# Gate and up of two chunks per feed-forward block as seven block products instead of eight

## The chip, the core and the metric

The kernel runs on one core of a Trainium2 chip. Its engines are TensorE (in the profile PE, with its weight loads as PEld), VectorE (DVE), ScalarE (ACT), GpSimd (POOL) and SyncE (SP), which here only issues the transfers of weights. The metric is the device time of one execution in microseconds (us); lower is better.

## The reference, cut to what matters

Two layers, each with a feed-forward block, a mixer (latent attention with a recurrence in the first layer, differential attention in the second), and a second feed-forward block: four feed-forward blocks in all. The sequence has 256 tokens of width 1024; all inputs are fp32.

```python
def swiglu(x, w_gate, w_up, w_down):
    return (jax.nn.silu(x @ w_gate) * (x @ w_up)) @ w_down
...
    h = swiglu(rms_norm(x, g[0, 0]), ffn_w_gate[l, 0], ffn_w_up[l, 0], ffn_w_down[l, 0])
    x = x + 0.5 * rms_norm(h, g[0, 1])
```

`w_gate` and `w_up` are [1024, 2816], `w_down` is [2816, 1024], and each block has its own.

## The kernel before, in words

**Tiles.** The 256 tokens are two row tiles (t = 0, 1) of 128. The operand of a block stands in SBUF transposed, `xT[t]`, eight k tiles of [128, 128]. An fp32 product is made of three fp32r products: every value is split in a high part, `hi`, and a rest, `lo`, and `mm3` (lines 242 to 246) issues hi times hi, hi times lo and lo times hi, each a matmul of 512 columns into one PSUM bank.

**The weight stream.** All weights are stored in the order of use and pass through SBUF in subunits of [128, 1024] fp32 (512 KB). `emit_load` (line 197) emits for each: the transfer into a tile `raw` (pool of 5), the copy to `hi` by ScalarE (line 219) and the rest `lo` = `raw` - `hi` by VectorE (line 224), the rests in the order of the stream. In a feed-forward block the pairs `hi`, `lo` take 7 places of a pool of the block's own (`BUFS_F`); subunits that are emitted ahead of the block's opening take the 5 places of the pool `wsp`. `fill` (line 256) keeps about seven subunits emitted ahead of TensorE.

**A feed-forward block** (`ffn`, line 430) goes over the 2816 columns in chunks of 512, 512, 256, 512, 512, 512. A chunk of 512 takes four subunits of gate and four of up, each of two k tiles; each subunit serves both row tiles: 2 tiles x 2 k tiles x 3 = 12 matmuls. Then ScalarE computes silu of gate, VectorE the product with up (`gated`, line 445), and one chunk later `turn` (line 448) transposes the result and splits it to `hT`, and `down` (line 454) multiplies it with four subunits of down, 12 matmuls each, into the four banks `y`. Chunk 0 is made by `group_first` (line 275): row tile 0 first, while the second tile's operand is still being normalised and transposed; chunks 1 to 5 by `group`. After the last chunk, `finish` (line 403) normalises the block's output and makes the next operand.

**Order.** The program is written once, unrolled; a scheduler places each engine's instructions in an order by priority (norms and the splits of transposes ahead), and each engine then runs its queue in that order. GpSimd has only small work in these blocks: one power of a [128, 1] column per norm (lines 343 and 388).

Of the kernel before, what the change touches and what calls it, by code (L numbers as in the profile page):

```python
# [20 lines left out]
P = 128  # L21
D = 1024
# [12 lines left out]
BUFS_F = 7  # L35
CHUNKS = [512, 512, 256, 512, 512, 512]

# ---------------------------------------------------------------- weight stream
# A unit is (name, index, first k tile, k tiles, column ranges): [128, k tiles, columns],
# stored contiguously in the order of use.  # L40


def _ffn_units(l, j):
# [12 lines left out]
    for ci, (a, w) in enumerate(starts):  # L56
        step = 2048 // w
        for k in range(0, KD, step):
# [54 lines left out]
for _i in range(1, len(UNITS)):  # L113
    if UNITS[_i - 1][0].endswith("w_out") and not UNITS[_i][0].endswith("w_out"):
        BLOCK_OF[_i - 1] = BLOCK_OF[_i]
        MOVED.add(_i - 1)
# [6 lines left out]
def _pack(inputs):  # L123
    parts = []
    for name, idx, k0, nk, cols in UNITS:
# [6 lines left out]
# ---------------------------------------------------------------- constants of the shapes  # L132
# [37 lines left out]
def forward(ctx, tc, a):  # L170
# [19 lines left out]
    # ------------------------------------------------------------ weight stream  # L190
    SPLIT = 1024
    state = {"i": 0, "off": 0, "block": -1, "pool": None, "first": None, "n": 0}
# [3 lines left out]

    def emit_load():
        if state["i"] >= len(UNITS):
            return
        u = UNITS[state["i"]]  # L200
        pool, tag = (state["pool"], "f") if BLOCK_OF[state["i"]] == state["block"] else (wsp, "w")
# [3 lines left out]
        off = state["off"]  # L205
        state["off"] += P * width
        src = a["w"][off:off + P * width].rearrange("(p n) -> p n", p=P)
        nc_ = width // nk
        per = max(1, SPLIT // nc_)
        for k in range(0, nk, per):  # L210
            n = min(per, nk - k)
            w = n * nc_
            raw = wraw.tile([P, SPLIT], F32, name="raw", tag="raw")
            moved = nc.sync.dma_start(raw[:, :w], src[:, k * nc_:k * nc_ + w])
            if state["n"] in late:
                after(late[state["n"]](), moved)
# [13 lines left out]
    def take(nk):  # L230
        """The next subunits that make up nk k tiles."""
# [10 lines left out]
    def mm3(ps, lhs, j, rhi, rlo, start, stop):  # L242
        hi, lo = lhs
        mm(ps, hi[:, j, :], rhi, start=start, stop=False)  # L244
        mm(ps, hi[:, j, :], rlo, start=False, stop=False)  # L245
        state["mm"] = mm(ps, lo[:, j, :], rhi, start=False, stop=stop)  # L246
# [16 lines left out]
    def group(pss, lhss, n, nk=KD, k0=0):  # L263
        """pss[t][:, :n] = lhs_t^T @ the next weight group [nk*128, n]; a step of side work after each subunit."""
# [46 lines left out]
    # ------------------------------------------------------------ start  # L311
# [19 lines left out]
    def after(b, a_):  # L331
        """b is issued after a_ (on one engine)."""
# [5 lines left out]
    def rpow(ss, n, mul, add):  # L338
        """(ss * mul + add) ** -0.5"""
# [6 lines left out]
    def to_T(src, dst, n, j0=0, bank=bank):  # L346
        """dst[(hi, lo)][:, j0:j0+n, :] = transposes of the n 128-column blocks of src."""
# [15 lines left out]
    def turn_x(t, xg):  # L363
        """Closures: halves of xT[t] = xg^T, split."""
# [11 lines left out]
    def post_norm(t, ys, g, half, gnext):  # L376
        """x[t] += (0.5 if half) rms(y) g; returns xg = x[t] * gnext."""
# [40 lines left out]
    # ------------------------------------------------------------ FFN  # L418
    def ffn_scope(block):
        """Opens the pools of an FFN; its weights go to them from here on."""  # L420
# [6 lines left out]
        state["tmp"] = lambda: fp.tile([P, 512], F32, name="tmp", tag="h")  # L427
        return fx, fp, fr

    def ffn(scope, r, turn1, gpost, gnext, at=None):  # L430
        fx, fp, fr = scope
        with fx:
# [21 lines left out]
            def down(t, subs, first, last, k0=0, banks=(0, 1)):  # L454
                """y[t] += h^T ^T @ the down weights; first/last: the f tile that opens/closes the sum."""
                for hi, lo, m, _ in subs:
# [4 lines left out]
                    k0 += m  # L461

# [10 lines left out]
            h = [gated(t, pu[t], s[t], w) for t in range(NT)]  # L473
            for ci in range(1, nch):
                w, wp = CHUNKS[ci], CHUNKS[ci - 1]
                pg = [bank(), bank()]
# [41 lines left out]
    # ------------------------------------------------------------ rope tables  # L518
# [39 lines left out]
    def rope(v, tab, w, pool):  # L558
        """v [P, n, 2w] in place; tab [P, 2, 2w] = (cos cos), (-sin sin)."""
# [13 lines left out]
    # ------------------------------------------------------------ output projection of a mixer  # L573
# [46 lines left out]
    def even(r, turn1, tab, lb, lbm):  # L620
        with ExitStack() as ex:
# [23 lines left out]
            def turn4(src, dst, rows=P, w=P, copy=None, bank=bank):  # L645
                """dst [rows, 4, P] = transposes of the four w-column blocks of src."""
# [5 lines left out]
            # ---- latent q and rope part of k  # L652
# [29 lines left out]
            # ---- latent kv  # L682
# [14 lines left out]
            # ---- forget gate  # L697
# [471 lines left out]
```

## Time and profile before

| | |
|---|---|
| device time, median of 3 runs | 1028.74 us (1028.34 to 1030.66) |
| span of the profiled execution, first to last instruction | 1027.8 us |
| PE busy | 1011.3 us, 98% of the span, 4979 matmuls |
| DVE busy | 625.8 us, 61% |
| ACT busy | 517.1 us, 50% |
| POOL busy | 49.9 us, 5% |
| weight stream, mean of all transfers | 179 GB/s |

The profiled execution has no time of its own beside its span; the median of the runs is 0.94 us above the span. Matmuls are pipelined, so their listed durations overlap; the rate of TensorE is read from start to start. [...]

### The profile page before, as it was taken

What the parts mean: (1) busy time and instruction counts of PE and PEld (TensorE: products, weight loads), DVE (VectorE), ACT (ScalarE), POOL (GpSimd) and SP (SyncE); (2) the same over time, 40 slices, a digit from 0 to 9 for tenths busy, and PEclk for the clock granted to TensorE, in tenths of its full rate; (3) what the DMA queues carried; (4) which work ended last, traced back from release to release, by engine and by line L of the source; (5) the groups of instructions that cost most, each with busy time, mean ns of one, the idle gap of its engine ahead of it and who ended that gap; (6) DMA issues with size and microseconds to landing.
All of it is one profiled execution on the core that took longest, in us unless ns stands there. A gap on an engine that the chain in (4) does not pass through costs nothing.

```text
span 1027.8 us, 13158 instructions
## 1 busy us (share of the span) xinstructions
PE 1011.3 (98%) x4979; PEld 843.5 (82%) x4979; DVE 625.8 (61%) x876; ACT 517.1 (50%) x757; POOL 49.9 (5%) x61
## 2 busy tenths in 40 slices
PE   8999999999999999999999999999999999999997
PEld 6888888888788889888888888888877878888886
DVE  6555585768577855455576555546676786455553
ACT  6544455477644644444554444444665565444441
POOL 1000000021201000000000000000011200000000
PEclk8999999999999999999999999999999999999999
DMA  8765555575221765555547555555634366655531
GB/s 282 271 202 186 186 184 189 180 225 194 86 81 58 253 212 196 185 184 187 182 164 246 187 183 189 191 190 168 208 121 147 102 206 225 201 182 189 186 123 41
DMA packets 51903, 184.25 MB, mean 179 GB/s; under 512 B 6136, under 2 KB 6528, under 8 KB 51840
## 3 DMA queue, kind: packets, MB, share of 16 engines
q1 hardware_dynamic: 48960, 176.05, 51.8%
q10 hardware_dynamic: 2880, 7.37, 2.1%
q8 instruction: 39, 0.64, 0.2%
q14 instruction: 24, 0.20, 0.1%
HBM read 182.35 MB, written 1.05 MB: 178 GB/s over the span
## 4 chain that ended last, share of the span: by engine, by line
PE 90%; DVE 4%; issue 3%; ACT 1%; DMA 1%; POOL 1%; SPq 0%; DVEq 0%; POOLq 0%; ACTq 0%
PE w L244 16%; PE w L246 16%; PE w L245 16%; PE y L246 9%; PE y L244 9%; PE y L245 9%; PE w L292 7%; PE w L353 2%; DVE wlo L224 1%; PE y L353 1%; DMA raw<-in_w_dram 1%; ACT whi L219 1%; POOL pm L1007 0%; DVE E L857 0%; DVE pm L1009 0%
## 5 line engine op out<-in xcount | busy, mean ns | idle before, releaser
L224 DVE TENSOR_TENSOR wlo<-raw,whi 128x1024 fp32r<-128x1024 f32 (+2 forms) x331 | 404.0, 1227 | 283.6 <-ACT whi L219 281.2
L219 ACT CAST whi<-raw 128x1024 fp32r<-128x1024 f32 (+1 forms) x331 | 345.0, 1049 | 365.5 <-PE w L246 206.6
L244 PE MATMUL w<-whi,xThi 128*128 128x512 f32 (+1 forms) x836 | 315.6, 377 | 0.0
L246 PE MATMUL w<-whi,xTlo 128*128 128x512 f32 (+1 forms) x836 | 312.0, 373 | 0.0
L245 PE MATMUL w<-wlo,xThi 128*128 128x512 f32 (+1 forms) x836 | 311.5, 373 | 0.0
L246 PEld LDWEIGHTS w<-whi,xTlo 128*128 128x128 f32 x836 | 157.3, 188 | 28.3 <-issue 0.3
L244 PEld LDWEIGHTS w<-whi,xThi 128*128 128x128 f32 x836 | 157.5, 188 | 27.5 <-issue 1.0
L245 PEld LDWEIGHTS w<-wlo,xThi 128*128 128x128 f32 x836 | 157.5, 188 | 26.4
L244 PE MATMUL y<-whi,hThi 128*128 128x512 f32 x352 | 138.4, 393 | 0.0
L246 PE MATMUL y<-whi,hTlo 128*128 128x512 f32 x352 | 137.2, 390 | 0.0
L245 PE MATMUL y<-wlo,hThi 128*128 128x512 f32 x352 | 137.1, 389 | 0.0
L246 PEld LDWEIGHTS y<-whi,hTlo 128*128 128x128 f32 x352 | 66.1, 188 | 14.0
L245 PEld LDWEIGHTS y<-wlo,hThi 128*128 128x128 f32 x352 | 66.1, 188 | 13.2
L244 PEld LDWEIGHTS y<-whi,hThi 128*128 128x128 f32 x352 | 66.1, 188 | 13.2
L361 DVE TENSOR_TENSOR hTlo<-w,hThi 128x512 fp32r<-128x512 f32 (+1 forms) x48 | 29.1, 640 | 34.0 <-ACT hThi L360 34.0
L440 ACT ACTIVATE s<-w,sm 128x512 f32<-128x512 f32 (+1 forms) x48 | 31.4, 653 | 25.9 <-PE w L246 20.3
L388 POOL TENSOR_TENSOR sm<-sm,mhalf 128x1 f32<-128x1 f32 x12 | 6.6, 550 | 726.6 <-DVE sm L386 726.6
L292 PE MATMUL w<-whi,xThi 128*128 128x512 f32 (+2 forms) x124 | 39.1, 397 | 2.6 <-ACT xThi L360 2.6
L292 PE MATMUL w<-wlo,xThi 128*128 128x512 f32 (+2 forms) x124 | 37.8, 389 | 0.4 <-DVE wlo L224 0.4
L292 PE MATMUL w<-whi,xTlo 128*128 128x512 f32 (+2 forms) x124 | 37.9, 390 | 0.0
L445 DVE SCALAR_TENSOR_TENSOR h<-w,sm,s 128x512 f32<-128x512 f32 (+1 forms) x48 | 32.0, 699 | 0.7 <-PE w L246 0.5
L292 PEld LDWEIGHTS w<-whi,xThi 128*128 128x128 f32 x124 | 22.6, 192 | 6.6 <-ACT xThi L360 3.1
(246 smaller groups left out, 820.2 us busy)
## 6 DMA issues: line engine op xcount, KB each, us to landing
raw<-in_w_dram SPq DMA_DIRECT2D x325, 512.0 KB, 3.6
g<-in_norm_g_dram ACTq DMA_DIRECT2D x9, 512.0 KB, 4.6
raw<-in_w_dram SPq DMA_DIRECT2D x4, 448.0 KB, 3.4
g<-in_norm_g_dram SPq DMA_DIRECT2D x2, 512.0 KB, 6.2
out_dram<-x SPq DMA_DIRECT2D x4, 256.0 KB, 2.1
E<-in_hw_dram ACTq DMA_DIRECT2D x1, 576.0 KB, 6.7
x<-in_x_dram SPq DMA_DIRECT2D x2, 256.0 KB, 3.0
x<-in_x_dram SPq DMA_DIRECT2D x1, 512.0 KB
```

What stands on the lines that cost most here:

```text
L219: c = nc.scalar.copy(hi[:, :w], raw[:, :w])
L224: state["lo"] = nc.vector.tensor_tensor(lo[:, :w], raw[:, :w], hi[:, :w].bitcast(F32), op=ALU.subtract)
L244: mm(ps, hi[:, j, :], rhi, start=start, stop=False)
L245: mm(ps, hi[:, j, :], rlo, start=False, stop=False)
L246: state["mm"] = mm(ps, lo[:, j, :], rhi, start=False, stop=stop)
L292: state["mm"] = mm(o, lhs[:, k, :], rhs[:, i, :], start=j == 0 and k == 0, stop=j == 2 and k == KD - 1)
L353: nc.tensor.transpose(ps[:, i * P:(i + 1) * P], src[:, (b + i) * P:(b + i + 1) * P], ident)
L361: return c, nc.vector.tensor_tensor(lo.rearrange("p a b -> p (a b)"), ps, h2.bitcast(F32), op=ALU.subtract)
L388: nc.gpsimd.tensor_tensor(r, v, mhalf[:, :1], op=ALU.pow)
L440: nc.scalar.activation(s[:, :w], ps[:, :w], AF.Silu, scale=r[t])
L445: nc.vector.scalar_tensor_tensor(hh[:, :w], ps[:, :w], r[t], s[:, :w], op0=ALU.mult, op1=ALU.mult)
```

## The change: what it does

In chunks 1 and 3 of each block (`SEVEN = (1,3)`), gate and up are taken as one product of 2 x 2 blocks: row tile times half of k, and half of k times {gate, up}, each block of weights [512, 512]. Strassen's scheme in Winograd's form makes it from seven block products (`prod`, 12 matmuls each) instead of eight:

- Four sums of rows of the operand, `row_sums`, once per block after chunk 0: twelve GpSimd operations on [128, 512] (four re-additions of `hi` and `lo`, four sums, four rests) and four ScalarE copies. Both chunks use them.
- Four sums of weights per chunk (T1 to T4), each of two subunits: eight VectorE operations on [128, 1024], made in place in the `raw` tiles, which come from a pool of 8 of their own.
- Each of the seven weight blocks is split as before: 14 subunits with `hi` and `lo` instead of 8. A subunit now serves one product, 6 matmuls instead of 12.
- The products are added in PSUM where they can be (banks X, W, Y), with three ScalarE copies (`held`) and three VectorE sums (`plus`) per chunk for the rest.
- The down products of the chunk before are taken between the products T3 and T4 and after B22.
- The pairs `hi`, `lo` of a block take, by turns (`RING`), the 5 places of `wsp` and 4 of the block's own: 9 in all.

```diff
-BUFS_F = 7
+BUFS_F = 4
+SEVEN = (1,3)
+RAWS = 8
+RING = "wfwfwfwfw"
...
+        if ci in SEVEN:
+            gate, up = ([("ffn_w_" + n, (l, j), k, 4, [(a, a + w)]) for k in (0, 4)] for n in ("gate", "up"))
...
+            units += [gate[0] + ("B11",), up[0] + ("T1",), up[1] + ("T2",), gate[1] + ("B21",), (None, None, 0, 4, [(a, a + w)], "T3")]
+            units += d[:half] + [(None, None, 0, 4, [(a, a + w)], "T4"), (None, None, 0, 4, [(a, a + w)], "B22")] + d[half:]
+            continue
...
+                raw = (wraw if kind is None else state["raws"]).tile([P, SPLIT], F32, name="raw", tag="raw")
...
+                sub = nc.vector.tensor_tensor
+                if kind in ("B11", "B21"):
+                    kept[kind, k] = raw
+                elif kind == "T1":
+                    sub(raw, raw, kept["B11", k], op=ALU.subtract)
+                    kept["T", k] = raw
+                elif kind == "T2":
+                    kept["B22", k] = raw
+                    sub(kept["T", k], raw, kept["T", k], op=ALU.subtract)
+                    raw = kept["T", k]
+                elif kind == "T3":
+                    raw = kept["B11", k]
+                    sub(raw, kept["T", k], raw, op=ALU.subtract)
+                elif kind == "T4":
+                    raw = kept["B21", k]
+                    sub(raw, raw, kept["T", k], op=ALU.subtract)
+                else:
+                    raw = kept["B22", k]
+            pool, tag = wsp, "w"
+            if ours:
+                if RING[state["turn"] % len(RING)] == "f":
+                    pool, tag = state["pool"], "f"
+                state["turn"] += 1
...
+            def row_sums(fp):
+                xf = [cp.tile([P, D], F32, name="xf", tag="c") for _ in range(NT)]
+                A = [[xf[t][:, 512 * i:512 * i + 512] for i in range(2)] for t in range(NT)]
+                tt = nc.gpsimd.tensor_tensor
+                for t in range(NT):
+                    for i in range(2):
+                        hi, lo = (v.rearrange("p k n -> p (k n)").bitcast(F32) for v in half(t, i))
+                        tt(A[t][i], hi, lo, op=ALU.add)
+                tt(A[1][1], A[1][0], A[1][1], op=ALU.add)
+                tt(A[1][0], A[0][0], A[1][0], op=ALU.subtract)
+                tt(A[0][0], A[1][1], A[0][0], op=ALU.subtract)
+                tt(A[0][1], A[0][1], A[0][0], op=ALU.subtract)
...
+                for v, dst in zip((A[1][1], A[0][0], A[1][0], A[0][1]), (oT[0], oT[1], *more)):
+                    hi, lo = (d.rearrange("p k n -> p (k n)") for d in dst)
+                    nc.scalar.copy(hi, v)
+                    tt(lo, v, hi.bitcast(F32), op=ALU.subtract)
...
+                X = bank()
+                prod(X, half(0, 0), True)
+                hT = [turn(0, CHUNKS[ci - 1]), None]
+                W = bank()
+                prod(W, S1, True)
+                p1 = held(X)
+                hT[1] = turn(1, CHUNKS[ci - 1])
+                prod(X, S2, False)
+                Y = bank()
+                prod(Y, half(0, 1), True)
+                u2 = held(X)
+                s0 = silu(0, plus(p1, Y), 512)
+                prod(X, S3, False)
+                downs(range(kf))
+                u3 = held(X)
+                c22 = plus(u3, W)
+                prod(X, half(1, 1), False)
+                s1 = silu(1, X, 512)
+                prod(W, S4, False)
+                h = [gated(0, plus(u2, W), s0, 512), gated(1, c22, s1, 512)]
+                downs(range(kf, wp))
...
+            sums = row_sums(fp)
             for ci in range(1, nch):
                 w, wp = CHUNKS[ci], CHUNKS[ci - 1]
+                if ci in SEVEN:
+                    seven(ci)
+                    continue
```

## Rows read from the trace of the kernel before

**Rows 1.** The page, part 1: busy us, share of span, instructions of each engine.

```profile
PE 1011.3 (98%) x4979; PEld 843.5 (82%) x4979; DVE 625.8 (61%) x876; ACT 517.1 (50%) x757; POOL 49.9 (5%) x61
```

**Rows 2.** The page, part 4: the chain that ended last, by engine.

```profile
PE 90%; DVE 4%; issue 3%; ACT 1%; DMA 1%; POOL 1%; SPq 0%; DVEq 0%; POOLq 0%; ACTq 0%
```

**Rows 3.** Timeline of PE, a gate group: start us, us, instruction, count [idle before].

```profile
450.90 0.39 PE L244 MATMUL w<-whi,xThi 128*128 128x512 f32 x1
...
461.78 1.03 PE L353 MATMUL w<-ident,h 128*128 128x128 f32 x8
462.57 0.47 PE L244 MATMUL w<-whi,xThi 128*128 128x512 f32 x1
```

**Rows 4.** Groups by shape: busy us, mean ns of one | idle before, releasers.

```profile
L224 DVE TENSOR_TENSOR wlo<-raw,whi 128x1024 fp32r<-128x1024 f32 x325 | 398.3, 1231 | 283.6 <-ACT whi L219 281.2
L219 ACT CAST whi<-raw 128x1024 fp32r<-128x1024 f32 x325 | 340.2, 1053 | 362.0 <-PE w L246 206.6 <-PE y L246 101.9 <-issue 24.5
...
L360 ACT CAST hThi<-w 128x512 fp32r<-128x512 f32 x40 | 21.7, 588 | 4.7 <-PE w L353 4.6
...
L385 DVE TENSOR_TENSOR c<-y,g 128x512 f32<-128x512 f32 x12 | 8.2, 684 | 6.1 <-ACT junk L383 6.1
```

**Rows 5.** Timeline of PE at the third feed-forward block's start and its chunk 1.

```profile
530.77 0.62 PE L292 MATMUL w<-whi,xThi 128*128 128x512 f32 x2
...
553.50 0.39 PE L244 MATMUL w<-whi,xThi 128*128 128x512 f32 x1
```

**Rows 6.** Timeline of DVE in the same block, around chunks 0 and 1.

```profile
539.31 0.69 DVE L361 TENSOR_TENSOR xTlo<-y,xThi 128x512 fp32r<-128x512 f32 x1 [2.10 <-ACT xThi L360]
541.21 6.90 DVE L224 TENSOR_TENSOR wlo<-raw,whi 128x1024 fp32r<-128x1024 f32 x6 [1.20 <-ACT whi L219]
...
554.97 1.40 DVE L445 SCALAR_TENSOR_TENSOR h<-w,sm,s 128x512 f32<-128x512 f32 x2
...
565.78 1.29 DVE L361 TENSOR_TENSOR hTlo<-w,hThi 128x512 fp32r<-128x512 f32 x2 [1.61 <-ACT hThi L360]
```

**Rows 7.** Timeline of ACT at the same place.

```profile
539.17 2.00 ACT L219 CAST whi<-raw 128x1024 fp32r<-128x1024 f32 x2
```

**Rows 8.** Timeline of POOL in the first mixer: two places with dense operands.

```profile
234.80 1.37 POOL L709 TENSOR_TENSOR E<-lb,E 128x512 f32<-128x512 f32 x1
...
307.95 2.61 POOL L909 TENSOR_TENSOR G<-G,gout 128x512 f32<-128x512 f32 x2 [1.17 <-ACT G L908]
```

**Rows 9.** Timeline of DVE at the same two places.

```profile
234.93 2.32 DVE L224 TENSOR_TENSOR wlo<-raw,whi 128x1024 fp32r<-128x1024 f32 x1
...
307.87 0.28 DVE L857 TENSOR_TENSOR E<-E,hqT 128x128 f32<-128x128 f32 x1
308.07 1.37 DVE L857 TENSOR_TENSOR E<-E,hkT 128x128 f32<-128x128 f32 x1
309.36 1.35 DVE L857 TENSOR_TENSOR E<-E,hqT 128x128 f32<-128x128 f32 x1
```

**Rows 10.** Groups by shape, POOL alone, the dense [128, 512] operations.

```profile
L909 POOL TENSOR_TENSOR G<-G,gout 128x512 f32<-128x512 f32 x2 | 2.6, 1326 | 1.2 <-ACT G L908 1.2
L708 POOL TENSOR_TENSOR E<-E,lbm 128x512 f32<-128x512 f32 x2 | 2.6, 1290 | 4.8 <-DVE kk L707 4.8
```

**Rows 11.** Windows: stretch, length, busy us (count) by engine, PEclk, DMA share, GB/s.

```profile
530.77:545.34 14.57, 14.57 (x69) 12.04 (x68) 9.39 (x14) 8.90 (x13) 1.10 (x2) 1.00 0.31 111
545.34:553.50 8.16, 8.16 (x37) 6.76 (x36) 5.21 (x5) 3.92 (x4) 0.00 (x0) 1.00 0.96 306
...
553.50:576.30 22.80, 22.80 (x106) 18.96 (x105) 13.86 (x14) 10.96 (x13) 0.00 (x0) 1.00 0.71 235
```

**Rows 12.** Windows and timeline of PE at the program's start.

```profile
9.00:12.00 3.00, 2.57 (x6) 1.50 (x7) 3.00 (x4) 2.46 (x3) 0.00 (x0) 0.50 1.02 419
...
8.92 1.18 PE L292 MATMUL w<-whi,xThi 128*128 128x512 f32 x2 [2.64 <-ACT xThi L360]
...
16.73 0.62 PE L292 MATMUL w<-whi,xTlo 128*128 128x512 f32 x2
```

More of the change, by code (lines that the diff above doesn't have):

```diff
@@ L113 @@
 for _i in range(1, len(UNITS)):
-    if UNITS[_i - 1][0].endswith("w_out") and not UNITS[_i][0].endswith("w_out"):
+    if (UNITS[_i - 1][0] or "").endswith("w_out") and not (UNITS[_i][0] or "").endswith("w_out"):
         BLOCK_OF[_i - 1] = BLOCK_OF[_i]
@@ L191, in forward @@
     SPLIT = 1024
-    state = {"i": 0, "off": 0, "block": -1, "pool": None, "first": None, "n": 0}
+    state = {"i": 0, "off": 0, "block": -1, "pool": None, "first": None, "n": 0, "turn": 0}
     queue = []
@@ L195, in forward @@
     late = {}
+    kept = {}
     def emit_load():
@@ L200, in emit_load @@
         u = UNITS[state["i"]]
-        pool, tag = (state["pool"], "f") if BLOCK_OF[state["i"]] == state["block"] else (wsp, "w")
+        ours = BLOCK_OF[state["i"]] == state["block"]
         state["i"] += 1
@@ L204, in emit_load @@
         nk = u[3]
-        off = state["off"]
-        state["off"] += P * width
-        src = a["w"][off:off + P * width].rearrange("(p n) -> p n", p=P)
+        kind = u[5] if len(u) > 5 else None
+        if u[0] is not None:
+            off = state["off"]
+            state["off"] += P * width
+            src = a["w"][off:off + P * width].rearrange("(p n) -> p n", p=P)
         nc_ = width // nk
@@ L212, in emit_load @@
             w = n * nc_
[L213 to L216, printed above, removed]
+            if u[0] is not None:
+                raw = (wraw if kind is None else state["raws"]).tile([P, SPLIT], F32, name="raw", tag="raw")
+                moved = nc.sync.dma_start(raw[:, :w], src[:, k * nc_:k * nc_ + w])
+                for key in [key for key in late if key <= state["n"]]:
+                    after(late.pop(key)(), moved)
+            if kind is not None:
+                sub = nc.vector.tensor_tensor
[21 more added lines that the diff above has]
+                state["turn"] += 1
             hi = pool.tile([P, SPLIT], F32R, name="whi", tag=tag + "hi")
@@ L461, in down, with half @@
                     k0 += m
+            def half(t, i):
+                return tuple(v[:, 4 * i:4 * i + 4, :] for v in xT[t])
+            def row_sums(fp):
[10 more added lines that the diff above has]
+                tt(A[0][1], A[0][1], A[0][0], op=ALU.subtract)
+                more = [tuple(fp.tile([P, 4, P], F32R, name=f"S{n}{i}", bufs=1) for n in ("hi", "lo")) for i in range(2)]
+                out = []
+                for v, dst in zip((A[1][1], A[0][0], A[1][0], A[0][1]), (oT[0], oT[1], *more)):
+                    hi, lo = (d.rearrange("p k n -> p (k n)") for d in dst)
+                    nc.scalar.copy(hi, v)
+                    tt(lo, v, hi.bitcast(F32), op=ALU.subtract)
+                    out.append(dst)
+                return out
@@ new lines, in prod, with seven, held, plus @@
+            def prod(ps, lhs, start):
+                k0 = 0
+                while k0 < 4:
+                    fill()
+                    hi, lo, m, _ = queue.pop(0)
+                    for i in range(m):
+                        k = k0 + i
+                        mm3(ps, lhs, k, hi[:, i, :], lo[:, i, :], start and k == 0, k == 3, not start)
+                    k0 += m
+                    pump()
+            def seven(ci):
+                nonlocal h, hT
+                wp = CHUNKS[ci - 1] // P
+                kf = (wp // 2 + 1) // 2 * 2 if ci < nch - 1 else 0
+                wp = wp if ci < nch - 1 else 0
+                S1, S2, S3, S4 = sums
+                def held(ps):
+                    c = fp.tile([P, 512], F32, name="u", tag="u", bufs=2)
+                    nc.scalar.copy(c, ps)
+                    return c
+                def plus(c, ps):
+                    nc.vector.tensor_tensor(c, ps, c, op=ALU.add)
+                    return c
+                def downs(ks):
+                    for k in ks:
+                        sub = take(1)
+                        for t in range(NT):
+                            down(t, sub, 0 if ci == 1 else None, None, k)
+                X = bank()
[19 more added lines that the diff above has]
+                downs(range(kf, wp))
```

19 lines of the change are left out of this document (13 added, 6 removed).

## The prediction

> **What bounds the kernel now.** I read the page's first part before anything else: TensorE is busy for 1011.3 of 1027.8 us, VectorE for 61%, ScalarE for 50%, GpSimd for 5% [rows 1]. The chain that ended last says the same with more weight: 90% of it is TensorE [rows 2]. Busy time alone does not say whether TensorE runs at its pace, so the next view is its timeline: 48 matmuls of a gate group lie between 450.90 and 461.78, start to start 10.88 / 48 = 0.2267 us, and the eight transposes behind them cost 0.79 us [rows 3]. That is a dense queue at granted clock 1.00. A matmul taken out is worth 0.227 us, as long as weights keep arriving split. Who makes them: per subunit one ScalarE copy of 1.05 us and one VectorE rest of 1.23 us [rows 4], against the 12 x 0.227 = 2.72 us that TensorE needs for a subunit. Both engines mostly wait; VectorE's rests wait for the copy, the copies for TensorE to free a place [rows 4].
>
> **What is removed.** Each of two chunks in each of four blocks loses one block product of 12 matmuls: 12 x 0.2267 = 2.72 us a chunk, 5.44 a block, 21.8 in all. Nothing is added on TensorE: matmuls and transposes keep their shapes.
>
> **What is added, on VectorE.** In a chunk of seven products a subunit feeds 6 matmuls, 1.36 us of TensorE. VectorE owes for it a rest, and for the eight subunits of T1 to T4 a sum as well. I price the sum like the rest, both being fp32 with two operands in SBUF: six rests back to back took 6.90 us, so (6.90 - 1.22) / 5 = 1.135 us a step [rows 6]. A sum and a rest are then 2.27 us against TensorE's 1.36: here VectorE is the slower engine, and what counts is how far ahead it enters. I do the ledger for the third block, whose operation times I have.
>
> TensorE's side: chunk 0 starts at 530.77, chunk 1 at 553.50 [rows 5]. B11, T1, T2, B21 take 4 x 2.72 = 10.88, the transposes 0.79, the first subunit of T3 1.36; the second subunit of T3 is due at 553.50 + 13.03 = 566.53.
>
> VectorE's side: at 541.21 the rests of the block's subunits begin again, with the sixth, because its copy (done at 541.17 [rows 7]) needs the place of the first, in use until row tile 1 has passed it. Numbered from 0, subunits 5 to 17 need 13 rests. Of the six sums to T3 I take the two of T1 as done earlier: VectorE idles 2.10 and 1.20 us there [rows 6], and their weights can have landed, since the transfers ran at 111 GB/s in 530.77:545.34 and reached 306 behind it [rows 11]. That leaves 17 x 1.135 = 19.30; then the gated products 1.40 and the two splits 1.29 [rows 6], and one `plus`, priced at 0.68 like a sum from PSUM [rows 4]. Together 22.67: done at 563.88, 2.65 us early. If no T1 sum is early, it is 0.4 us early. So without GpSimd the saving survives, barely.
>
> **What is added, on GpSimd, decides.** Twelve operations on [128, 512] a block, on an engine that is idle there. The trace shows what such an operation does to its neighbour. At 307.95 two of them take 2.61 us [rows 8]; of the VectorE products beside them, 0.28 us each, two take 1.37 and 1.35 [rows 9]. At 234.80 one of 1.37 us runs [rows 8], and the weight rest started at 234.93 takes 2.32 us instead of 1.23 [rows 4, 9]. Each GpSimd operation takes about 1.09 us from a VectorE operation with two operands in SBUF, and rests and sums are all of that kind. GpSimd's own length is 1.29 to 1.33 us [rows 10]. The bounds are 0 (all in VectorE's waits) and 12 x 1.09 = 13.1 us a block. I take nine, 9.8 us: the two re-additions of row tile 0 and the first of row tile 1 can run before 541.21, the others need the last half of `xT[1]` (539.31 + 0.69 [rows 6]) and fall on the stretch of the ledger. So T3 is late by 9.81 - 2.65 = 7.16 us, and the block changes by 7.16 - 5.44 = +1.7; break-even lies at (2.65 + 5.44) / 9 = 0.90 us an operation.
>
> Behind T3 nothing more is lost: four rests, two sums and two rests of T4 and B22 and one sum, 8 x 1.135 + 0.68 = 9.8 us, stand against 1.36 + 5.44 + 2.72 + 1.36 = 10.9 of TensorE. Chunk 3 uses the same row sums; before it lies chunk 2 with 22 us of TensorE for some 15 of VectorE, so I cost it at nothing. Cover gone, it would cost what chunk 1 does without GpSimd.
>
> [...]
>
> **Smaller edits.** ScalarE gets 6 copies a chunk (6.3 us), three held copies (3 x 0.59 [rows 4]) and once four copies of row sums; it was busy for 10.96 of 22.80 us there [rows 11], so it is not the slower one: 0, at most what VectorE's order adds. Transfers keep their bytes; 8 raw tiles of their own let SP issue them earlier: 0, between -1 and +1 a block. Held copies lie beside a product or down products (2.72 us or more for 0.59): 0. At the three block ends with a successor the next block's first pairs share the five `wsp` places with the last down subunits, and two early GpSimd operations meet the norm's VectorE work: I take one operation's worth, +1 us each, between 0 and 2. In the first block the tables of angles, some small VectorE work, move from beside chunk 3's end toward its start, since a chunk of seven steps 14 times and not 8: 0 to 3, taken 0.
>
> **The sum.** Four blocks x 1.7 = +6.9, three ends x 1 = +3.0. On the profiled span: 1027.8 + 9.9 = 1037.7; the runs' median lies 0.94 above that span, so 1038.6. The ends: no meeting on the port and no loss at ends, 1028.7 - 21.8 = 1007; all twelve meet and no sum is early, 13.1 - 0.4 - 5.44 = +7.3 a block and 2 an end, 1064.
>
> **Rivals.**
> A, faster: GpSimd's operations fall into VectorE's waits. For: VectorE is busy only 13.86 of 22.80 us there now [rows 11]. Against: those waits are what the new sums fill, and both begin when `xT[1]` is there. Then 1028.7 - 21.8 + 3 = 1010; 1007 to 1020.
> B, level: fewer meet. With seven, T3 is late by 7.63 - 2.65 = 4.98, the block at -0.5, in all 1030; 1022 to 1031.
> C, clearly slower: the lateness comes in one piece and TensorE's clock falls. The program's start shows it: 2.64 us of idle, then a granted clock of 0.50, two matmuls in 1.18 us at 8.92 and in 0.62 again at 16.73 [rows 12]. At half rate from 8.92 to 16.2, 7.3 us, TensorE loses 3.6; four times is 14.5: 1038.6 + 14.5 = 1053. It decides if one wait of TensorE in chunk 1 passes about 2.6 us: a gated product queued on VectorE behind sums that wait, with the transposes behind it. Against: if each subunit waits about 1 us, the clock stays, as with the 0.79 us of short transposes. [...]
> D, that the change doesn't do what it says: then TensorE would not have 4979 - 96 = 4883 matmuls. I see nothing for it.
>
> **Chances.** Forecast 0.42 (1031 to 1047, itself), A 0.30, B 0.13, C 0.15. A is all faster; B splits 0.03 faster, 0.06 level, 0.04 slower; of the forecast 0.03 is level. Faster by over 0.2% (2 us, about what a measurement of this kernel can tell from no change) 0.33, within 0.09, slower 0.58. The range runs from A's middle to C's, 1010 to 1053, which leaves about 0.2 outside.
>
> **What would show it.** Right: TensorE idle in chunk 1 of each block, ended by VectorE's rests, sums or gated products, about 7 us a block; rests and sums beside GpSimd of about 2.3 us; chunk 3 dense. Wrong: GpSimd's row sums beside VectorE operations of plain length; TensorE waiting as long in chunk 3 as in chunk 1; waits that end with a transfer or a ScalarE copy whose source had long been there.

## The result, and the profile after

The changed kernel takes 1067.68 us (median of 4 runs, 1067.12 to 1068.34) against 1028.97 for the kernel before (4 runs on the same chip, 1028.34 to 1030.66): 1.0371 times as long, 95% interval 1.0355 to 1.0388. The forecast was 1038.6, with a range from 1010 to 1053. The direction was right, the size was not: +38.7 us in place of +9.9. The profiled execution of the changed kernel has a span of 1065.7 us, 37.9 more than before.

The page's first part, which answers to [rows 1], and the chain by engine, which answers to [rows 2]:

```profile
PE 1005.6 (94%) x4883; PEld 833.1 (78%) x4883; DVE 805.3 (76%) x1012; ACT 582.9 (55%) x845; POOL 151.1 (14%) x109
...
PE 69%; DVE 15%; issue 7%; DMA 3%; ACT 3%; POOL 2%; SPq 0%; DVEq 0%; POOLq 0%; ACTq 0%
```

TensorE has 96 matmuls fewer, as it should (rival D is out), but its share of the chain fell from 90% to 69%. Where, the windows of the third block show, chunks 0 to 3 (stretch, length, busy us and count of PE, PEld, DVE, ACT, POOL, then granted clock, which is the share of TensorE's full clock in the records, DMA share, GB/s), first before (its chunk 0 is in [rows 11], in two pieces), chunks 1 to 3:

```profile
553.50:587.06 33.56, 33.56 (x153) 27.85 (x152) 19.75 (x19) 15.18 (x17) 0.00 (x0) 1.00 0.67 222
587.06:610.34 23.28, 23.28 (x153) 21.39 (x152) 11.88 (x12) 10.22 (x12) 0.00 (x0) 1.00 0.54 181
610.34:638.04 27.70, 27.70 (x126) 22.91 (x124) 14.33 (x14) 12.36 (x14) 0.00 (x0) 1.00 0.57 190
```

then after, chunks 0 to 3:

```profile
552.74:577.55 24.81, 22.96 (x105) 18.72 (x104) 21.62 (x17) 13.67 (x20) 18.38 (x12) 1.00 0.46 149
577.55:618.79 41.24, 33.13 (x142) 27.11 (x140) 39.06 (x36) 23.79 (x28) 5.70 (x3) 0.88 0.53 179
618.79:642.07 23.28, 23.28 (x154) 21.39 (x152) 22.55 (x24) 12.06 (x14) 0.00 (x0) 1.00 0.36 136
642.07:667.05 24.98, 24.98 (x113) 20.62 (x112) 20.50 (x20) 19.55 (x23) 0.00 (x0) 1.00 0.56 189
```

Chunk 3 has its 2.72 us to the last digit. Chunk 1 is 7.7 us longer, with VectorE busy for 39.06 of 41.24 and the clock at 0.88. The same cut through all four blocks (start of a chunk's first product to start of the next chunk's), summed, against the terms of the forecast:

| us against before | forecast | measured |
|---|---|---|
| chunk 3 | -10.9 | -10.6 |
| chunk 1 | 4 x (7.16 - 2.72) = +17.8 | +33.7 |
| chunk 0, mixers, start | +3.0 | +10.7, +0.5, +1.6 |
| all the rest | 0 | +2.0 |
| sum | +9.9 | +37.9 |

In chunk 1 the extra is of two kinds. Waits of TensorE add 34.6 us (four long ones, 10.0, 8.3, 8.3 and 7.2 us above a matmul's step, and a short one), and matmuls slower than 0.3 us from start to start, most of them behind a wait, add 8.1; against that stand 10.9 us saved, and 1.9 lie in smaller steps. This is the long wait in the third block, on PE's timeline:

```profile
580.05 0.39 PE L293 MATMUL w<-whi,xTlo 128*128 128x512 f32 x1
588.54 1.08 PE L400 MATMUL w<-ident,h 128*128 128x128 f32 x4 [8.11 <-DVE h L494]
```

After the first product of the chunk, 2.7 us into it, TensorE wants the transposes of chunk 0's `h`, and `h` is not there. VectorE's timeline over the same time says why:

```profile
564.76 15.15 DVE L271 TENSOR_TENSOR wlo<-raw,whi 128x1024 fp32r<-128x1024 f32 x7 [0.70 <-ACT whi L266]
579.83 4.50 DVE L249 TENSOR_TENSOR raw<-raw 128x1024 f32<-128x1024 f32 x2
584.25 1.21 DVE L253 TENSOR_TENSOR raw<-raw 128x1024 f32<-128x1024 f32 x1
585.39 2.35 DVE L271 TENSOR_TENSOR wlo<-raw,whi 128x1024 fp32r<-128x1024 f32 x2
587.66 1.40 DVE L494 SCALAR_TENSOR_TENSOR h<-w,sm,s 128x512 f32<-128x512 f32 x2
```

Seven rests take 15.15 us, 2.16 a step, where six took 6.90 before [rows 6]. Behind them the two sums of T2, a sum of T3 and two rests stand ahead of the two gated products in VectorE's queue. GpSimd's timeline beside it:

```profile
565.51 2.15 POOL L525 TENSOR_TENSOR xf<-xf 128x512 f32<-128x512 f32 x1
...
574.33 4.49 POOL L534 TENSOR_TENSOR oTlo<-xf,oThi 128x512 fp32r<-128x512 f32 x2
578.79 4.46 POOL L534 TENSOR_TENSOR Slo<-xf,Shi 128x512 fp32r<-128x512 f32 x2
```

Beside the rests each operation of the row sums takes 2.15 to 2.25 us, and one VectorE step goes by in the same time. And the granted clock around the wait (windows, columns as above):

```profile
580.00:588.00 8.00, 0.44 (x2) 0.01 (x1) 8.00 (x6) 5.41 (x6) 3.25 (x2) 0.67 0.00 0
588.00:590.00 2.00, 1.46 (x6) 1.39 (x7) 2.00 (x3) 0.34 (x1) 0.00 (x0) 0.50 0.00 0
590.00:592.00 2.00, 2.00 (x7) 1.51 (x6) 1.90 (x3) 1.20 (x2) 0.00 (x0) 0.50 0.00 0
592.00:594.00 2.00, 2.00 (x9) 1.58 (x8) 2.00 (x3) 0.00 (x0) 0.00 (x0) 0.75 0.00 0
594.00:596.00 2.00, 2.00 (x13) 1.71 (x11) 1.27 (x3) 1.51 (x3) 0.00 (x0) 1.00 0.77 233
```

TensorE comes back at a granted clock of 0.50 and gets 1.00 again some 5 us later. The DMA share is 0 through the wait and for some five more microseconds: no transfer runs. The waits of SyncE, which issues the transfers, name the reason (575 to 602: us in total, times, longest):

```profile
SPq L237 <- DVE wlo L271: 24.8, 5, 21.9
```

For 21.9 us in one piece the next transfer waits for a rest on VectorE, that is, for a raw tile to come free.

### The profile page after: what moved, and what is told of

It reads as the page before. It is cut to its first block, busy times and chain, and to the rows that moved or that the text cites. A ratio compares the mean times of both kernels' runs of the same rounds, so it can differ in the third digit from the quotient of the medians.

```text
span 1065.7 us, 13235 instructions
## 1 busy us (share of the span) xinstructions
PE 1005.6 (94%) x4883; PEld 833.1 (78%) x4883; DVE 805.3 (76%) x1012; ACT 582.9 (55%) x845; POOL 151.1 (14%) x109
## 4 chain that ended last, share of the span: by engine, by line
PE 69%; DVE 15%; issue 7%; DMA 3%; ACT 3%; POOL 2%; SPq 0%; DVEq 0%; POOLq 0%; ACTq 0%
PE w L291 13%; PE w L293 12%; PE w L292 12%; DVE wlo L271 8%; PE y L291 7%; PE y L293 7%; PE y L292 7%; DMA raw<-in_w_dram 3%; PE w L339 3%; PE w L400 2%; ACT whi L266 1%; PE w L1010 1%; DVE x L441 1%; DVE raw L249 1%; POOL sm L390 1%
## 5 line engine op out<-in xcount | busy, mean ns | idle before, releaser
L271 DVE TENSOR_TENSOR wlo<-raw,whi 128x1024 fp32r<-128x1024 f32 (+2 forms) x379 | 488.6, 1315 | 119.5 <-ACT whi L266 117.2
L266 ACT CAST whi<-raw 128x1024 fp32r<-128x1024 f32 (+2 forms) x379 | 391.2, 1048 | 281.9 <-PE w L293 106.4
L291 PE MATMUL w<-whi,xThi 128*128 128x512 f32 (+1 forms) x676 | 252.7, 374 | 1.0 <-ACT s L489 1.0
L293 PE MATMUL w<-whi,xTlo 128*128 128x512 f32 (+1 forms) x676 | 249.5, 369 | 0.0
L292 PE MATMUL w<-wlo,xThi 128*128 128x512 f32 (+1 forms) x676 | 249.2, 369 | 0.0
L291 PEld LDWEIGHTS w<-whi,xThi 128*128 128x128 f32 x676 | 127.4, 189 | 22.8 <-ACT s L489 1.2
L293 PEld LDWEIGHTS w<-whi,xTlo 128*128 128x128 f32 x676 | 127.3, 188 | 22.1 <-issue 0.3
L292 PEld LDWEIGHTS w<-wlo,xThi 128*128 128x128 f32 x676 | 127.5, 189 | 20.4
L293 PEld LDWEIGHTS y<-whi,hTlo 128*128 128x128 f32 x352 | 66.1, 188 | 14.3
L400 PE MATMUL w<-ident,h 128*128 128x128 f32 x176 | 27.0, 286 | 33.2 <-DVE h L494 26.1
L408 DVE TENSOR_TENSOR hTlo<-w,hThi 128x512 fp32r<-128x512 f32 (+1 forms) x48 | 29.8, 643 | 33.2 <-ACT hThi L407 33.1
L407 ACT CAST hThi<-w 128x512 fp32r<-128x512 f32 (+1 forms) x48 | 25.2, 554 | 52.1 <-PE w L400 52.1
```

Of the source, the lines that this page charges most:

```text
L266: c = nc.scalar.copy(hi[:, :w], raw[:, :w])
L271: state["lo"] = nc.vector.tensor_tensor(lo[:, :w], raw[:, :w], hi[:, :w].bitcast(F32), op=ALU.subtract)
L291: mm(ps, hi[:, j, :], rhi, start=start, stop=False, skip_group_check=again)
L292: mm(ps, hi[:, j, :], rlo, start=False, stop=False, skip_group_check=again)
L400: nc.tensor.transpose(ps[:, i * P:(i + 1) * P], src[:, (b + i) * P:(b + i + 1) * P], ident)
L407: c = nc.scalar.copy(h2, ps)
```

## The experiments

Theory V: VectorE, slowed by the row sums on GpSimd, has too much to do before chunk 1. Rivals: the order of the queues alone (O, later Q), late weights and the rings of places (W, R). All times are medians of four runs or more beside runs of the kernel before, in brackets the 95% interval of the ratio. "Chunk 1" and the like are sums over the four blocks against before.

**Which part makes it.**

Chunk 3 alone with seven products:

```diff
-SEVEN = (1,3)
+SEVEN = (3,)
```

> SEVEN = (3,): chunk 1 goes back to eight products, chunk 3 keeps seven, the row sums stay on GpSimd at the block's start. In the trace of the changed kernel chunk 1 is +7.4 to +9.5 us a block against before (33.9 in all), chunk 3 -2.5 to -2.72 (10.7 in all), chunk 0 and the block starts +12 in all. Theory V (VectorE, slowed by GpSimd's row sums, is late for chunk 1): chunk 1 returns to 33.6 us in each block, chunk 3 stays at 24.98, the starts keep their +12 because the twelve GpSimd operations still lie there: 1029 - 10.7 + 12 = 1030. Theory S (the starts are longer through the shared ring of pairs and the earlier demand of chunk 1 of seven, not through GpSimd): starts back to before, 1029 - 10.8 = 1018. If the shared row sums or the ring hurt later chunks too: above 1040.

1058.19 us, 1.0272 (1.0254 to 1.0290). Neither V nor S, but the case named last: chunk 3 gives its 10.6, and chunk 1, which has eight products again and the matmuls of before, is still 25.0 us longer. So chunk 1 needs no sums of weights of its own for a loss there.

No row sums:

```diff
-            sums = row_sums(fp)
+            sums = [half(0, 0), half(0, 1), half(1, 0), half(1, 1)]
```

> The row sums are left out: products S1 to S4 take the four halves of the operand as they stand, so gate and up of chunks 1 and 3 are not the reference's; all matmuls, weight sums, rests and rings stay. Theory V: without twelve GpSimd operations VectorE gets back about 12 x 1.03 = 12 us a block between chunk 0 and chunk 1 (its rest went from 1.135 to 2.16 us a step beside them), more than the 8 to 10 us by which the transposes waited; the wait goes, the clock stays, the starts lose their +12: 1068 - 34 - 10 - 12 = about 1010, at most 1020. Theory O (VectorE's order alone: the gated product stands behind the sums of T2 and T3 whatever GpSimd does): the three operations ahead of it still cost 3 x 1.135 + 2 x 1.17, so a wait of 3 us or more per block and the clock's fall stay: 1035 to 1045. Theory W (weights land late, places in the rings): nothing much changes, above 1050.

1024.61 us, 0.9946 (0.9931 to 0.9962). Chunk 1 is 7.6 us shorter than before, so 41.2 shorter than in the changed kernel: V. This edit takes the four ScalarE copies of the row sums out as well; but in the changed kernel VectorE works without a gap up to the gated products of chunk 0 (in the third block from 564.76 to 587.66, in the others as long), so these copies did not hold it up there. The total stays above V's 1020 because chunk 0 (+7.1) and the mixers (+3.3) did not come back, which neither theory had said.

Four of the twelve GpSimd operations left out:

```diff
-                    tt(lo, v, hi.bitcast(F32), op=ALU.subtract)
-                    out.append(dst)
+                    out.append((dst[0], half(0, 0)[1]))
```

> The changed kernel with eight GpSimd operations a block instead of twelve: the rests of the four row sums are left out (products S1 to S4 take a half of the operand's rest in their place, so gate and up of chunks 1 and 3 are not the reference's). Theory V (each operation takes 1.04 us of VectorE, and all of it is TensorE's wait): 4 x 1.04 x 4 blocks = 16.6 us back, and more where a wait becomes short enough for the clock to stay: 1043 to 1051. Theory O (the order of VectorE's queue decides, the last operations come too late to matter): above 1060.

1050.82 us, 1.0195 (1.0167 to 1.0222), as V said. Chunk 1 gives back 18.1 us, 1.1 for each of the 16 operations, and here the ScalarE copies stay. All 48 together, with the copies, gave 41.2, 0.86 each.

The twelve operations on VectorE:

```diff
-                tt = nc.gpsimd.tensor_tensor
+                tt = nc.vector.tensor_tensor
```

> The twelve row-sum operations run on VectorE instead of GpSimd, nothing else changes. Theory V: on GpSimd they took about 12 us from VectorE; on VectorE they cost 12 x 0.69 = 8.3 us (the price of a 512-column operation there). VectorE gains 4 us a block, some of it also at the starts, 12 to 20 us in all: 1048 to 1056. Theory O: VectorE has 8.3 us more to do in the same order, and no partner was slowing it: 1068 + 4 x 8 = 1100.

1042.87 us, 1.0138 (1.0105 to 1.0172): 24.8 us better than on GpSimd, more than V said. Chunk 1 is +17.9, chunk 0 +2.4. The engine that was to be spared is better off doing the work itself. The transposes hardly wait for the gated products any more (1.6 us in one wait); what is left in chunk 1 is mostly the row sums being late for the second product, S1: TensorE waits for their ScalarE copies `oThi` three times, 10.9 us in all.

**Order or work.** The T2 sums behind the gated products:

```diff
+            for b in sums2[-2:]:
+                after(b, state["h"])
             sums = row_sums(fp)
```

> The two sums of T2 in each chunk of seven, and what follows them on VectorE, are ordered behind the gated products of the chunk before; the work is the same. Theory O (order alone): the transposes no longer wait, all of the 34 us of long waits and the 10 us of half clock go: 1068 - 44 = 1024 to 1030. Theory V (VectorE has 7 us a block too much work before T3, wherever it stands): the wait moves from the transposes to the products of T2 and T3. VectorE was busy without a pause from 564.76 to about 594 in the third block; T3's second rest could not come before 597.5, against 590.4 when it would be due without the wait: 7.1 us late as before, so only the share of the clock can come back, up to 2.4 us a block, if the lateness comes in pieces: 1058 to 1068.

1060.09 us, 1.0288 (1.0264 to 1.0311). Order gives about 7 us, no more: chunk 1 goes from +33.7 to +27.5, of which about 1.0 is two matmuls of chunk 2 in each block that this order takes early. PE's timeline of the third block shows the wait in its new places, both behind ScalarE copies, which V had not named:

```profile
583.18 0.50 PE L292 MATMUL w<-whi,xThi 128*128 128x512 f32 x1 [2.90 <-DVE hTlo L409]
585.54 0.80 PE L292 MATMUL w<-whi,oThi 128*128 128x512 f32 x1 [1.86 <-ACT u L561]
```

The split `hTlo` is late since its copy stands on ScalarE behind a copy of T2 that waits for VectorE. So that copy was moved too:

```diff
                 hT = [turn(0, CHUNKS[ci - 1]), None]
+                for b in casts2[-2:]:
+                    after(b, state["hc"])
```

> The changed kernel with the sums of T2 behind the gated products (as in the run before, 1060.1) and the copies of T2 behind the copy of the first transposes (hThi of row tile 0), which in that run stood behind a copy that waited 8.45 us for VectorE. Same work, only the order on VectorE and ScalarE. Theory Q (in the changed kernel too the loss is what stands ahead in the queues): the waits of chunk 1 go, 1068 - 34 - 10 = 1024 to 1035. Theory V (VectorE has too much to do before T2 and T3: from 575.6 in the third block two gated products, two sums, two rests and two splits, 8.6 us with GpSimd's share, stand before the product of T2, due 3.5 us after the first transposes): a wait of 3 to 5 us a block stays, now at T2, with the half clock behind it: 1048 to 1058.

1077.90 us, 1.0457 (1.0439 to 1.0474), a miss of both theories. In chunk 1 it is +29.8, with the same two matmuls, against +27.5 in the run before. The waits there end with rests of weights (11.2 us over four blocks), as V says, and as much with the ScalarE copies `u` of products (10.8), which V does not say. Most of the loss beyond the run before is this edit's own: it holds in chunk 3 too, which goes from -10.6 to +6.2. That copies made early before now wait for the transposes there is my reading.

**Place.** Chunk 3 alone, `row_sums(fp)` written behind chunk 1:

```diff
+                if ci == 2:
+                    sums = row_sums(fp)
```

> Seven products in chunk 3 alone, the row sums still on GpSimd but written behind chunk 1, so that they run beside chunk 2. With the row sums at the block's start the same kernel took 1058.2, chunk 1 (of eight products) being 25 us longer in all. Theory V (place decides: the rests beside GpSimd double, and only where VectorE has no lead does TensorE wait): chunk 2 has 23.3 us of TensorE for 11.9 of VectorE and 12 x 1.04 = 12.5 lost, with nine pairs in hand: chunk 1 back to 33.6, chunk 2 at most +1, chunk 3 -2.7: 1029 - 10.8 + 0 to 8 for the starts = 1018 to 1026. Rival G (GpSimd's toll falls on TensorE wherever it lies): 1045 to 1058.

1056.23 us, 1.0252 (1.0232 to 1.0271), and it tests nothing: GpSimd's queue was empty and the operands were there, so the operations started at the block's start as before. With a wait that holds them back:

```diff
-                        tt(A[t][i], hi, lo, op=ALU.add)
+                        b = tt(A[t][i], hi, lo, op=ALU.add)
+                        tc.add_manual_dep(b.ins, state["h"].ins.name, mybir.DependencyInfo(mybir.DependencyClass.Sync, mybir.DependencyReason.SCHED_ONLY), reason="late")
```

> As the run with seven products in chunk 3 alone and late row sums, but now the four re-additions on GpSimd wait for the gated product of chunk 1, so that the twelve operations really run beside the end of chunk 1 and chunk 2 (there they started at the block's start all the same, being ready). Theory V (place decides): chunk 0 +1 to +3 in all, chunk 1 back to 33.6 us in each block, chunk 2 at most +1, chunk 3 -2.7: 1029 - 10.8 + 2 to 6 = 1020 to 1025. Rival G (the toll falls on TensorE wherever the operations lie): 1040 to 1056.

1037.10 us, 1.0073 (1.0056 to 1.0090), between the two. Chunk 0 is +2.1 and chunk 1 +0.2, as V said, but chunk 2 is +14.3. That is not the toll of the operations on VectorE's: seven of the twelve ran while VectorE was idle, and took 1.3 us each. Third block, ScalarE:

```profile
590.45 0.62 ACT L534 CAST oThi<-xf 128x512 fp32r<-128x512 f32 x1 [5.82 <-POOL xf L526]
...
595.69 0.62 ACT L534 CAST Shi<-xf 128x512 fp32r<-128x512 f32 x1 [1.89 <-POOL xf L529]
596.22 3.89 ACT L266 CAST whi<-raw 128x1024 fp32r<-128x1024 f32 x4
600.01 0.83 ACT L489 ACTIVATE s<-w,sm 128x256 f32<-128x256 f32 x2
```

GpSimd, VectorE and PE:

```profile
595.62 1.30 POOL L535 TENSOR_TENSOR Slo<-xf,Shi 128x512 fp32r<-128x512 f32 x1
...
597.30 7.57 DVE L271 TENSOR_TENSOR wlo<-raw,whi 128x1024 fp32r<-128x1024 f32 x5 [10.65 <-ACT whi L266]
...
600.53 0.39 PE L291 MATMUL w<-whi,xThi 128*128 128x256 f32 x1 [2.22 <-ACT s L489]
```

The four copies of the row sums wait on ScalarE for GpSimd; the copies of four weights stand behind them, and chunk 2's silus behind those. VectorE idles for 10.65 us, and TensorE waits for the silu, in all four blocks (8.6 us in all). So this run shows that the operations' place can be changed, but it does not decide between V and G: it lost by order, on ScalarE.

**Why chunk 1 loses 25 us with eight products.** The ring of nine pairs alone, with no row sums and no chunk of seven:

```diff
-SEVEN = (1,3)
+SEVEN = ()
...
-            sums = row_sums(fp)
```

> SEVEN = () and no row sums: all chunks with eight products, as before; what is left of the change is the ring of nine pairs by turns from two pools in place of seven of the block's own. Chunk 0 and the mixer's end ahead of it were 7.1 and 3.3 us longer without row sums (the run that left them out), 2.5 of it in block 2, 4.2 + 2.4 around block 4. Theory R (the ring that a block shares with the mixer's last subunits): the same here, 1029 + 7 to 10 = 1036 to 1039. Theory P (the weight sums pull VectorE's work forward into chunk 0, not the ring): 1028 to 1031.

1033.92 us, 1.0039 (1.0024 to 1.0054), between the two: chunk 0 +0.7, chunk 1 +0.3, the rest spread over mixers and start. Then the row sums alone, with seven pairs of the block's own:

```diff
-BUFS_F = 4
-SEVEN = (1,3)
-RING = "wfwfwfwfw"
+BUFS_F = 7
+SEVEN = ()
+RING = "f"
```

> No chunk with seven products, seven pairs of the block's own as before, no T blocks: the kernel before, with the twelve GpSimd operations and four copies of the row sums at the place of the changed kernel, their results unused. Theory V (GpSimd's neighbours alone make the loss at chunks 0 and 1): chunk 0 +9 to +11 and chunk 1 +20 to +25 in all, as with chunk 3 alone: 1029 + 30 to 36 = 1059 to 1065. Theory O or W (it takes the sums of T, the new order or the ring as well): VectorE has 14 us of slack in chunk 1 and swallows 12: 1029 to 1038.

1037.95 us, 1.0079 (1.0054 to 1.0103). Against V: chunk 0 is +5.3, chunk 1 +0.3. Five rests take 10.17 us here too, and TensorE hardly notices (chunk 1). Then both together:

```diff
-SEVEN = (1,3)
+SEVEN = ()
```

> No chunk with seven products, but both the ring of nine pairs and the row sums on GpSimd with unused results. The ring alone took 1033.9 (chunk 1 +0.3 us), the row sums alone, with seven pairs as before, 1038.0 (chunk 0 +5.3, chunk 1 +0.3), chunk 3 alone, with both, 1058.2 (chunk 1 +25). Theory Q (the two meet: VectorE is 10 us behind through the row sums, and with nine pairs ScalarE's queue has two more copies of weights ahead of chunk 1's silus, 16 in place of 14, each waiting for a late transfer): chunk 1 +18 to +25 again, 1029 + 5 + 5 to 10 + 20 = 1055 to 1062. Rival T (it takes the chunk of seven and its raw tiles too): chunk 1 under +5, 1036 to 1042.

1063.54 us, 1.0307 (1.0282 to 1.0333), Q and a little more: chunk 1 +21.8, chunk 0 +10.9. Two edits that cost 0.3 us each in chunk 1 cost 21.8 together. ScalarE's timeline of the run with chunk 3 alone, third block, shows where they meet:

```profile
580.51 1.06 ACT L266 CAST whi<-raw 128x1024 fp32r<-128x1024 f32 x1 [0.79 <-DMA raw<-in_w_dram]
582.38 1.05 ACT L266 CAST whi<-raw 128x1024 fp32r<-128x1024 f32 x1 [0.81 <-DMA raw<-in_w_dram]
584.99 1.04 ACT L266 CAST whi<-raw 128x1024 fp32r<-128x1024 f32 x1 [1.56 <-DMA raw<-in_w_dram]
585.94 1.26 ACT L489 ACTIVATE s<-w,sm 128x512 f32<-128x512 f32 x2
```

and PE's timeline who waits for it:

```profile
582.26 1.04 PE L400 MATMUL w<-ident,h 128*128 128x128 f32 x8
586.67 0.54 PE L291 MATMUL w<-whi,xThi 128*128 128x512 f32 x1 [3.38 <-ACT s L489]
```

Gate is done at 582.5, but chunk 1's two silus stand behind copies of later weights, whose transfers are late because VectorE gives the raw tiles back late. SyncE's waits in 559 to 586 name it:

```profile
SPq L237 <- DVE wlo L271: 30.6, 14, 11.1
```

TensorE needs the bank that the silus read. In the first block two more such copies stand ahead of the silus with the ring than without (20 and 18, counted from the program's start). The last test moves the silus ahead of some copies and changes nothing else:

```diff
                 s = [silu(t, pg[t], w) for t in range(NT)]
+                if ci == 1:
+                    for b in casts[-2:]:
+                        after(b, state["silu"])
```

> Seven products in chunk 3 alone, row sums on GpSimd at the block's start (1058.2, chunk 1 +25 us), but the silus of chunk 1 are ordered ahead of the last two copies of weights that are emitted by then, and so stand behind 12 copies, not 16. Work and transfers are the same. Theory Q (chunk 1's wait is the silus' place behind copies that wait for transfers): the waits of 3.4 to 5.2 us and the half clock behind them go, chunk 1 under +6 in all: 1033 to 1039. Rival V (VectorE is late by 10 us, whatever stands where: the next thing that is late is a weight's rest): chunk 1 stays above +15: 1048 to 1058.

1033.59 us, 1.0027 (1.0015 to 1.0039): chunk 1 +0.25 in place of +25.0. VectorE pays the toll as before (its timeline, third block),

```profile
556.89 8.39 DVE L273 TENSOR_TENSOR wlo<-raw,whi 128x1024 fp32r<-128x1024 f32 x4 [0.56 <-ACT whi L267]
```

four steps of 2.1 us, and TensorE has no wait in chunk 1 (ScalarE's timeline: now it is the silu that waits for gate):

```profile
562.97 1.05 ACT L267 CAST whi<-raw 128x1024 fp32r<-128x1024 f32 x1 [1.02 <-DMA raw<-in_w_dram]
568.22 0.69 ACT L491 ACTIVATE s<-w,sm 128x512 f32<-128x512 f32 x1 [4.20 <-PE w L295]
```

So with eight products in chunk 1 the loss was order. With seven it is mostly work: taking GpSimd's operations away gave 18 us for a third of them and 41 for all, and the two orders that were tried gave 7 us and nothing. That some third order would give more is not ruled out.

**A version that beats both.** Seven products in chunks 3 and 5, the row sums on VectorE, written behind chunk 1:

```diff
-SEVEN = (1,3)
+SEVEN = (3,5)
...
-                tt = nc.gpsimd.tensor_tensor
+                tt = nc.vector.tensor_tensor
...
+                if ci == 2:
+                    sums = row_sums(fp)
```

> Seven products in chunks 3 and 5 in place of 1 and 3, and the row sums on VectorE, written behind chunk 1. Theory V: chunk 2 gets 12 x 0.69 = 8.3 us more on VectorE (11.9 of 23.3 busy before), chunk 5 is entered with a lead, since chunk 4 needs 19 of 33.6 us of VectorE; both chunks give 2.7 us: 1029 - 21.7 + 0 to 8 for the starts = 1007 to 1015. Rival L (a chunk of seven with no down products between its products runs out of split weights: 14 rests, 8 sums, 3 additions and 2 splits are 28 us of VectorE against 19.8 of TensorE): chunk 5 longer by 3 to 6 us instead of shorter, 1030 to 1045.

1021.45 us, 0.9918 (0.9898 to 0.9937). Chunk 3 gives 10.6, chunk 5 with the rest of its block 9.1, and rival L is out; chunk 0 is +3.9, chunk 1 +1.7, the mixers +1.5. With the re-additions ordered behind chunk 1's gated product:

```diff
+                        tc.add_manual_dep(b.ins, state["h"].ins.name, mybir.DependencyInfo(mybir.DependencyClass.NoSync, mybir.DependencyReason.SCHED_ONLY), reason="late")
```

> As the run with seven products in chunks 3 and 5 and row sums on VectorE, with the re-additions ordered behind the gated product of chunk 1. In that run chunk 0 was still 3.9, chunk 1 1.7, the mixers 1.5 us longer, since VectorE took some of the sums early. Theory V: these go to 0.7, 0.3 and 1.3 as in the run with the rings alone, chunks 3 and 5 keep -20.7: 1029 - 20.7 + 3 to 5 = 1011 to 1014. Rival Q (the waits there come from transfers and ScalarE's queue, not from the row sums): 1018 to 1022 again.

1017.01 us (1013.73 to 1021.39), 0.9881 (0.9852 to 0.9910): the fastest of all, 3 to 6 us short of what V said. Chunk 0 is still +2.2, and chunk 5 with the rest of its block gives 9.3, not 10.9. Its interval overlaps that of the run before it, so what the order alone adds is not settled.

## Why the prediction was wrong

**What held.** The saving: 2.71 us in chunk 3 of three blocks, 2.47 in the first. Chunk 3 "at nothing": dense, with chunk 2 ahead of it holding 11.88 us of VectorE's work before the change, less than the 15 that the prediction took. The toll: 1.09 us an operation was taken from [rows 9], and rests beside GpSimd went from 1.135 to 2.16, 1.03 more. Nine operations in VectorE's way in the third block: of the twelve, two fell on the norm, one on nothing. GpSimd's place as the decider: without row sums the loss in chunk 1 is a gain. So did the step of 1.135 us: four rests without a GpSimd operation beside them, at 596.85 in the changed kernel, took 4.63 us, (4.63 - 1.22) / 3 = 1.137. A port, which the ends of the forecast name, no run shows; the runs show the price of the meeting, 1.03 us for the rest and some 0.9 for the GpSimd operation (last section).

**The step that failed first: the ledger's one due time.** It closed the account at T3's second subunit, 13 us into chunk 1, and found VectorE 7.16 us late there. But VectorE works in the order of its queue, and the gated products, counted in the ledger as 1.40 us of work, stood behind the sums of T2 and T3. Their due time is the transposes, 2.7 us into the chunk; before it was 10.9 ([rows 3] shows the transposes behind 48 gate matmuls, and they stay there in a chunk of eight). The lateness so came in one piece of 7 to 10 us. That is rival C, which got 0.15 and was argued away with "if each subunit waits about 1 us". Its condition (one wait over 2.6 us, a gated product behind sums that wait) was met in all four blocks; its price for the clock, 14.5, was even too high (8.1), and so was its bound, an estimate from one wait of 2.64 us [rows 12], since in a later run a wait of at most 2.2 us came ahead of 0.62 and 0.50 (last section); but the wait itself came 2.7 us into the chunk and left nothing of the lead that the ledger counted on. In the terms of the sum, chunk 1 missed by 15.9 us: the waits came to 34.6 in place of 4 x 7.16 = 28.6, the half clock, put at nothing, to 8.1, and small steps to 1.9. With the gated products moved ahead of the sums, about 7 of it came back. The traces show VectorE and ScalarE keeping the order of their queues in two cases above: the gated products come at 587.66, behind the sums and rests ahead of them, and the silus of the run with chunk 3 alone at 585.94, behind the copies, with gate done at 582.5.

**Second: edits priced one by one.** The prediction put ScalarE and the transfers at nothing and gave the shared places a price at the block ends only. For chunk 1 that was true of each edit alone (0.3 us for the ring, 0.3 for the row sums) and false together (21.8). This was measured with eight products in chunk 1; how much of it lies in chunk 1 of the changed kernel, no run separates. In the run with chunk 3 alone VectorE, slowed, gave raw tiles back late (SyncE waited 30.6 us for its rests in 559 to 586), so transfers were late, so copies on ScalarE were late (0.79, 0.81 and 1.56 us of waits for transfers), and so were the silus behind these copies (3.38 us of TensorE's wait). The rule in the prediction, that an engine busy for half of a stretch is not the slower one, does not cover that: ScalarE was busy for 23.79 of 41.24 us.

**Third: the block starts.** +1 each at three ends was forecast; chunk 0 measured +10.7 in all, +2.1 in the third block. There the two early re-additions meet the norm's VectorE work, as forecast, but both of its steps, on the path (VectorE's timeline of the changed kernel, the second pair without a neighbour):

```profile
555.35 1.78 DVE L441 SCALAR_TENSOR_TENSOR x<-c,sm,x 128x512 f32<-128x512 f32 x1
557.16 1.64 DVE L447 TENSOR_TENSOR xg<-x,g 128x512 f32<-128x512 f32 x1
558.72 0.74 DVE L441 SCALAR_TENSOR_TENSOR x<-c,sm,x 128x512 f32<-128x512 f32 x1
559.49 0.69 DVE L447 TENSOR_TENSOR xg<-x,g 128x512 f32<-128x512 f32 x1
```

1.04 + 0.95 is nearly all of the +2.1. Blocks 2 and 4, behind a mixer, lost 5.0 and 3.6. The row sums alone give 5.3 over all blocks, with the ring 10.9, the ring alone 0.7: again the two meet. The run without row sums still had +7.1 there; in its fourth block, which has 4.2 of it, the norm's sums of squares stand on ScalarE behind copies that waited for transfers. Which edit puts them there was not tried.

What stays open: how the 41 us of chunk 1 in the changed kernel divide. Order gave about 7, the half clock is 8.1 by the matmuls' steps, and the two overlap; the rest I put down to VectorE's work, but the dose was not quite even (0.86 us an operation over all twelve, 1.1 over the last four).

## What to carry to other kernels

A ledger of work needs a due time for every consumer, in the order of the queue, not one at the end: ask of each instruction that waits what stands behind it, and of each that is due what stands ahead. Price edits in pairs where one delays the giving back of buffers and the other lets a queue run further ahead (here 0.3 and 0.3 us in chunk 1, together 21.8). Work put on an idle engine whose operations slow the busy one's is not free (here 1.03 us of a rest for each operation), and writing it later did not make it run later here (1056.23 us with seven products in chunk 3 alone); a wait did (1037.10). Then look at what stands behind whatever waits for that engine, as the copies of weights did on ScalarE.

## What was new in the hardware's behaviour

The neighbours slowed each other. The prediction took 1.29 to 1.33 us for a GpSimd operation [rows 10]; beside VectorE's rests it takes 2.15 to 2.25, so that the twelve operations took 23.1 us in the third block, not 16. The two gated products, which read one operand from PSUM, took 1.40 us beside GpSimd (575.56, in the run with the T2 sums behind them), the same as without it. The price of an operation of 512 columns on GpSimd was 1.03 us for the VectorE rest beside it and some 0.9 for the operation itself. Half the clock came behind a shorter wait than the 2.64 us of [rows 12]: in the run with the row sums held back, a wait of TensorE of at most 2.2 us in chunk 2 was followed by a granted clock of 0.62 and 0.50, in blocks 2 to 4 and not in the first (windows, third block):

```profile
598.00:600.50 2.50, 0.31 (x3) 0.07 (x1) 2.50 (x2) 2.50 (x5) 2.38 (x2) 1.00 0.11 26
600.50:602.00 1.50, 1.47 (x8) 1.47 (x9) 1.50 (x2) 1.50 (x3) 0.00 (x0) 0.62 0.76 306
602.00:604.00 2.00, 2.00 (x11) 2.00 (x11) 2.00 (x3) 0.74 (x2) 0.00 (x0) 0.50 0.63 203
```
